# Dilated-attention loads and the inverse's stores issued from GpSimd, query halves exchanged, head norm over two iterations

## The chip, the cores and the metric

The kernel runs on one core of a Trainium2 chip. The metric is the device time of one execution in microseconds (us). Engines are named as in the profile: PE (TensorE matmul), DVE (VectorE), ACT (ScalarE), POOL (GpSimd), SP (SyncE, which here only issues DMAs). ACTq, SPq and POOLq are DMA issues that stand in those engines' instruction streams. Each engine executes its instructions in the order of the program.

## The reference, cut to what matters

Two transformer blocks on one sequence of 1024 tokens, width 1024. The second block's mixer has two halves, both 512 wide, which the kernel runs side by side.

```python
# half 1: dilated attention, 8 heads of 64; three branches (window, dilation) share one softmax
DILATED_BRANCHES = ((128, 1), (512, 4), (2048, 16))
outs = [_dilated_branch(qh, kh, vh, w, d) for (w, d) in DILATED_BRANCHES]
m_all = maximum of the three m
num = sum(exp(m - m_all)[..., None] * acc for (m, l, acc) in outs)
den = sum(exp(m - m_all) * l for (m, l, acc) in outs)
# half 2: RWKV7, 8 heads of 64, a recurrence over the 1024 tokens
sa    = einsum('bhij,bhj->bhi', state, kk_t)
state = state * w_t - sa[..., None] * b_t + v_t[..., None] * k_t
y     = einsum('bhij,bhj->bhi', state, r_t)
# then a norm of y within each head, gain, bias, bonus and gate
yn = (y - mean) * lax.rsqrt(var + GN_EPS)
out = (yn * gn_w + gn_b + bonus) * g
mixed = concatenate([rms_norm(attn), out]) @ w_out      # then the feed-forward layer
```

## The kernel before, in words

The change lies in `mixers`, from about 1320 to 1725 us of the span. Ahead of it are block one and the projections of block two; behind it `finish` (the output projection, the feed-forward layer), whose first matmuls (tile x) need every dilated head and every norm of the mixer's first half of tokens, and whose further ones need the rest.

The dilated half is done as eight heads' passes, t = 0 to 7 (two attention heads of 64 channels each, and one half of the queries; passes 4 to 7 see 1024 keys instead of 512). `dil_load(t)` brings keys (dk) and values (dqv); `dil_load_q(x)` brings 256 queries (dq), for x = 0 to 15, two to a pass, into one of two buffers. A pass has 4 blocks of 128 queries and in each two heads (m): score matmuls into sc (L1288, L1289; 192 in the whole stage), a masked maximum on DVE (L1292), the exponential on ACT (L1298), transposes (tp, L254), products with the values (pv, L431). The result is stored to da_d (L1309). These loads and stores stand in ACT's stream.

The RWKV half is done as eight units, n = 0 to 7. For each: `rwkv_local` (call it L0 to L7; PE L1326 and L1337) makes matrices AT, stores them to at_d and loads them back as Al in another layout (SPq L1344, L1346). `rwkv_inverse` inverts triangles on POOL: a copy, then 31 steps of one multiplication (Ut, L1363) and one subtraction (U, L1365), and four stores to ut_d (SPq L1368). `rwkv_solve` (V0 to V7) loads ut_d as TB (SPq L1408, a single buffer), copies OFF on POOL (L1402), and runs six groups of matmuls (L1417, L1445, L1446, L1454) for two quads of chunks. `rwkv_state` (S) is a chain of eight small steps, a matmul (L1480) and an addition on DVE (L1482) each. `rwkv_norm` transposes, centres, squares, takes the reciprocal root on POOL (rstdh, L172), scales (L1519), transposes back (tile e), gates and stores to rw_d. Local, inverse, solve, state and norm of five units (n, n-1, n-2, n-3, n-4) run in one iteration of the loop; AT, RHS and RQ have three buffers, so a unit's local needs the buffers of the solve three units back.

All this stands in a block whose instruction order is worked out when the program is built, from the code and a model of the engines; so a changed line moves instructions on every engine. The order is fixed then; nothing is reordered at run time.

Of the kernel before, what the change touches and what calls it, by code (L numbers as in the profile page):

```python
# [86 lines left out]
class Build:  # L87
# [1158 lines left out]
    def dil_load(self, t):  # L1246

        i, n = t % 4, (t // 4 + 1) * 512
        v = self.dpool.tile([128, NT, 128], F32, name="dqv")
        K = [self.dpool.tile([128, S], F32R, name="dk", bufs=2) for _ in range(2)]  # L1250
        for m in range(2):
            self.nc.scalar.dma_start(K[m][:, :n].bitcast(F32), self.dqk_d[i][:, 2 + m, :n])
        self.nc.scalar.dma_start(v[:, :n // 128], self.dv_d[i][:n].rearrange("(t p) c -> p t c", p=128))
        self.dil_kv[t] = K, v

    def dil_load_q(self, x):

        i, g = x // 2 % 4, x // 8 * 2 + x % 2
        qs = self.dil_q[x] = self.dpool.tile([128, 2, 2, 256], F32R, name="dq", bufs=2)
        for s in range(2):  # L1260
            src = self.dqk_d[i][s * 64:s * 64 + 64, 0:2, g * 256:g * 256 + 256]
            for h in range(2):
                self.nc.scalar.dma_start(qs[h * 64:h * 64 + 64, :, s].bitcast(F32), src)

    def dilated(self, t):
# [222 lines left out]
    def rwkv_norm(self, n, p, hf):  # L1488

        nc = self.nc  # L1490
        t0 = hf * 512
# [7 lines left out]
        ps = None
        yield 1.0  # L1500

        def keep(i, n, x):
            nonlocal ps
            ps = x
        self.transposes([YT[:, j * 128:j * 128 + 128] for j in range(4)], keep, tag=tag)
# [13 lines left out]
        nc.vector.tensor_mul(y3(y), y3(y), rs[:, :, None].to_broadcast([128, 8, 64]))  # L1519
        self.transposes([y[:, j * 128:j * 128 + 128] for j in range(4)], keep, tag=tag)  # L1520
        nc.vector.tensor_mul(wg, ps, wg)
        nc.vector.tensor_add(wg, wg, bg)
# [529 lines left out]
```

## Time and profile before

| | |
|---|---|
| time, median of 3 runs | 2496.82 us (2484.91 to 2497.03) |
| the profiled execution's own time | 2490.68 us |
| its span in the profile | 2488.8 us, mean granted TensorE clock 0.977 |
| busy in the span | PE 95%, DVE 60%, ACT 41%, POOL 12% |
| PE idle before an instruction, 1384 to 1435 us | 9.04 and 6.35 us at two places |

The times of the rows further down are microseconds from the start of the span of this one execution. A busy PE there is not PE at its peak, since matmuls are pipelined and their ends modelled; the distance between the starts of two groups is the better measure of a group's price.

### The profile page before, as it was taken

The numbers are of one execution on the slowest core, as the hardware profiler recorded it, in microseconds if no ns is written. First come the engines' busy times: TensorE is split into PE (matmuls) and PEld (weight loads), VectorE is DVE, ScalarE is ACT, GpSimd is POOL, SyncE is SP. The second block draws the span as 40 slices with busy tenths as digits, with TensorE's granted clock in tenths as the row PEclk, the third lists the DMA queues.
The fourth block names the chain that finished last, engine by engine and source line by source line (L and its number), as shares of the span: only waits on it lengthen the run. The fifth ranks groups of instructions, "written<-read, shape, count | busy, mean of one in ns | idle before, by whom it ended". The sixth has DMA issues, their size and how long they took to land.

```text
span 2488.8 us, 38514 instructions
## 1 busy us (share of the span) xinstructions
PE 2354.3 (95%) x14272; PEld 2080.8 (84%) x14272; DVE 1493.3 (60%) x3189; ACT 1016.8 (41%) x2212; POOL 286.5 (12%) x678
## 2 busy tenths in 40 slices
PE   7999999999999999899999699989999999899997
PEld 6989998898887799788899688988987878678776
DVE  5534375555445545376663366757676666678888
ACT  4323343434442235233342344445665444443333
POOL 1100000000001000111203645331000000000001
PEclk9999999999999999999999899999999999999999
DMA  3144222312214432245467676534455444443222
GB/s 126 45 141 137 78 59 71 91 41 90 78 52 169 152 123 81 64 118 161 131 185 201 167 171 182 148 94 149 153 161 178 147 128 140 153 135 127 68 78 100
DMA packets 370188, 303.38 MB, mean 122 GB/s; under 512 B 124304, under 2 KB 303632, under 8 KB 370000
## 3 DMA queue, kind: packets, MB, share of 16 engines
q1 hardware_dynamic: 343888, 272.60, 36.6%
q10 hardware_dynamic: 25472, 26.22, 3.6%
q8 instruction: 113, 1.85, 0.3%
q0 software_dynamic: 640, 2.10, 0.2%
q14 instruction: 75, 0.61, 0.1%
HBM read 208.82 MB, written 91.23 MB: 121 GB/s over the span
## 4 chain that ended last, share of the span: by engine, by line
PE 71%; DMA 10%; DVE 9%; ACT 4%; issue 3%; POOL 2%; SPq 1%; ACTq 0%; DVEq 0%; POOLq 0%
PE pj L199 33%; PE x L199 7%; PE z L199 5%; PE pv L431 4%; PE y L199 4%; PE tp L254 3%; DMA wr<-w_ffn_up 3%; DVE w L181 2%; PE ua L199 2%; PE Z L1417 1%; PE sc L778 1%; DMA Al<-at_d 1%; ACT w L163 1%; PE ub L199 1%; DMA wr<-w_out 1%
## 5 line engine op out<-in xcount | busy, mean ns | idle before, releaser
L199 PE MATMUL pj<-w,hT_hi 128*128 128x256 f32 (+2 forms) x2496 | 526.6, 305 | 11.3 <-DVE c L165 6.2
L199 PEld LDWEIGHTS pj<-w,hT_hi 128*128 128x128 f32 x2496 | 409.8, 193 | 18.5 <-DVE c L165 7.5
L199 PE MATMUL pj<-hT_hi,w 128*128 128x512 f32 (+1 forms) x1216 | 394.3, 399 | 9.8 <-DVE tg L922 6.4
L199 PE MATMUL pj<-w,hT_lo 128*128 128x256 f32 (+2 forms) x1248 | 373.6, 300 | 0.0
L181 DVE TENSOR_TENSOR w<-wr,w 128x1024 fp32r<-128x1024 f32 (+4 forms) x339 | 273.1, 832 | 114.1 <-ACT w L163 113.2
L163 ACT ACTIVATE w<-wr 128x1024 fp32r<-128x1024 f32 (+4 forms) x335 | 236.1, 740 | 233.3 <-PE z L199 69.0
L199 PEld LDWEIGHTS pj<-hT_hi,w 128*128 128x128 f32 (+1 forms) x1216 | 227.0, 188 | 60.9 <-ACT w L163 4.8
L199 PEld LDWEIGHTS pj<-w,hT_lo 128*128 128x128 f32 x1248 | 240.2, 192 | 1.0 <-issue 0.5
L199 PE MATMUL pj<-hT_lo,w 128*128 128x512 f32 (+1 forms) x608 | 240.0, 395 | 0.0
L172 POOL TENSOR_TENSOR rstd<-rs_t,mhalf 128x1 f32<-128x1 f32 x88 | 62.3, 712 | 1482.2 <-DVE rs_t L171 1429.0
L199 PE MATMUL z<-w 128*128 128x512 f32 x720 | 168.5, 394 | 5.6 <-DVE c L1927 4.8
L199 PEld LDWEIGHTS z<-w 128*128 128x128 f32 x720 | 136.5, 190 | 36.1 <-issue 4.3
L199 PE MATMUL y<-w 128*128 128x512 f32 x624 | 148.4, 397 | 15.4 <-ACT w L163 9.0
L199 PEld LDWEIGHTS y<-w 128*128 128x128 f32 x624 | 118.8, 192 | 43.7 <-ACT w L163 10.2
L199 PE MATMUL ua<-T,w 128*128 128x512 f32 x576 | 139.3, 393 | 5.3 <-DVE o L1859 2.3
L199 PEld LDWEIGHTS ua<-T,w 128*128 128x128 f32 x576 | 107.3, 189 | 32.3 <-issue 6.3
L199 PEld LDWEIGHTS pj<-hT_lo,w 128*128 128x128 f32 (+1 forms) x608 | 114.8, 189 | 22.7 <-issue 0.2
L408 DVE TENSOR_REDUCE mx<-sc 128x1 f32<-128x128 f32 (+7 forms) x96 | 70.9, 754 | 101.5 <-PE sc L416 100.9
L254 PE MATMUL tp<-ident,p 128*128 128x128 f32 x576 | 98.4, 279 | 6.8 <-ACT pt L163 5.7
L199 PE MATMUL x<-w,mix_hi 128*128 128x256 f32 x512 | 92.6, 284 | 0.0
L199 PE MATMUL x<-B,w 128*128 128x512 f32 x384 | 88.3, 390 | 0.0
L412 ACT ACTIVATE p<-sc,mx 128x128 f32<-128x128 f32 (+7 forms) x96 | 70.7, 739 | 36.5 <-DVE mx L409 34.6
(448 smaller groups left out, 4423.5 us busy)
## 6 DMA issues: line engine op xcount, KB each, us to landing
wr<-w_ffn_up SPq DMA_DIRECT2D x48, 512.0 KB, 4.5
wr<-u_d SPq DMA_DIRECT2D x32, 512.0 KB, 3.3
wr<-w_ffn_down SPq DMA_DIRECT2D x32, 512.0 KB, 3.6
wr<-w_in SPq DMA_DIRECT2D x28, 512.0 KB, 4.0
wr<-w_in_first SPq DMA_DIRECT2D x64, 192.0 KB, 2.7
u_d<-o SPq DMA_DIRECT2D x48, 256.0 KB, 3.0
tg<-tg_d SPq DMA_DIRECT2D x32, 256.0 KB, 2.8
x_d<-x SPq DMA_DIRECT2D x16, 512.0 KB, 3.9
```

Source lines behind the costliest of these rows:

```text
L163: self.nc.scalar.activation(out, in_, AF.Copy)
L172: nc.gpsimd.tensor_tensor(out, t, self.mhalf[:, :ss.shape[-1]], op=OP.pow)
L181: self.nc.vector.tensor_sub(lo, x, hi.bitcast(F32))
L199: self.nc.tensor.matmul(ps, a, b, start=start, stop=stop, **({"skip_group_check": True} if onto else {}))
L254: self.nc.tensor.transpose(tp[:, j * 128:j * 128 + 128], s, ident)
L408: nc.vector.tensor_reduce(mx, sc[:, :n], axis=AX, op=OP.max)
L412: nc.scalar.activation(p[:, :n], sc[:, :n], AF.Exp, bias=mx, scale=scale, accum_out=s)
L431: self.nc.tensor.matmul(o[:, :w], pts[j], V[:, j], start=j == 0, stop=j == nb - 1)
L778: nc.tensor.matmul(o, qn, KN[:, c0:c0 + w], start=True, stop=False)
L1417: mm(ps[:, j * 128:j * 128 + 128], lhs(c), rhs(c, j), start=True, stop=True)
```

## The change

Five edits. The loads of dk, dqv and dq and the stores of da_d are issued by POOL instead of ACT, and the stores of ut_d by POOL instead of SP. Keys come as tiles of 512 with four buffers, so that one DMA brings both heads' keys and the next pass's keys may be loaded early. A dq load is three DMAs instead of four: the 128 rows as they are, and the two halves exchanged; the second score matmul takes the exchanged copy. The load of the next 256 queries stands behind the first block's first scores, and da_d's store of a pass stands in the next pass. The norm is cut in two: `rwkv_norm` up to the reciprocal root in one iteration, `rwkv_out` (load of wb, scale, transposes, gate, store) in the next; the loop has one iteration more. Beside `rwkv_out` the diff's new helpers `centre` and `gate` hold DVE work that stood in `rwkv_norm`.

```diff
 def dil_load(self, t):
-    v = self.dpool.tile([128, NT, 128], F32, name="dqv")
-    K = [self.dpool.tile([128, S], F32R, name="dk", bufs=2) for _ in range(2)]
-    for m in range(2):
-        self.nc.scalar.dma_start(K[m][:, :n].bitcast(F32), self.dqk_d[i][:, 2 + m, :n])
-    self.nc.scalar.dma_start(v[:, :n // 128], self.dv_d[i][:n].rearrange("(t p) c -> p t c", p=128))
+    for c in range(n):
+        K.append(self.dpool.tile([128, 2, 512], F32R, name="dk", bufs=4))
+        self.nc.gpsimd.dma_start(K[c].bitcast(F32), self.dqk_d[i][:, 2:4, c * 512:c * 512 + 512])
+    v = self.dpool.tile([128, NT, 128], F32, name="dqv")
+    self.nc.gpsimd.dma_start(v[:, :n * 4], self.dv_d[i][:n * 512].rearrange("(t p) c -> p t c", p=128))
 def dil_load_q(self, x):
-    for s in range(2):
-        src = self.dqk_d[i][s * 64:s * 64 + 64, 0:2, g * 256:g * 256 + 256]
-        for h in range(2):
-            self.nc.scalar.dma_start(qs[h * 64:h * 64 + 64, :, s].bitcast(F32), src)
+    src = self.dqk_d[i][:, 0:2, g * 256:g * 256 + 256]
+    self.nc.gpsimd.dma_start(qs[:, 0].bitcast(F32), src)
+    for h in (0, 64):
+        self.nc.gpsimd.dma_start(qs[h:h + 64, 1].bitcast(F32), src[64 - h:128 - h])
 def dilated(self, t):
-                if x < 15:
-                    self.dil_load_q(x + 1)
-            if qb % 4 == 1 and t < 7:
-                self.dil_load(t + 1)
+            if qb % 4 == 1:
+                if t < 7:
+                    self.dil_load(t + 1)
+                if t > 0:
+                    self.dil_store.pop()()
-                    nc.tensor.matmul(sc[:, :w], q2[:, m, 0, q0:q0 + 128], K[m][:, c0:c0 + w], start=True, stop=False)
-                    nc.tensor.matmul(sc[:, :w], q2[:, m, 1, q0:q0 + 128], K[m][:, c0:c0 + w], start=False, stop=True)
+                    k = K[c0 // 512][:, m, c0 % 512:c0 % 512 + w]
+                    nc.tensor.matmul(sc[:, :w], q2[:, 0, m, q0:q0 + 128], k, start=True, stop=False)
+                    nc.tensor.matmul(sc[:, :w], q2[:, 1, m, q0:q0 + 128], k, start=False, stop=True)
-                            nc.scalar.dma_start(dst.rearrange("(t p) c -> p t c", p=128), o)
+                            put = lambda: nc.gpsimd.dma_start(dst.rearrange("(t p) c -> p t c", p=128), o)
+                            put() if t == 7 else self.dil_store.append(put)
                 yield back, 0.25 + n * 0.0036
+                if qb % 2 == 0 and m == 0 and x < 15:
+                    self.dil_load_q(x + 1)
 def rwkv_inverse(self, n, p, hf):
         for g in range(4):
-            nc.sync.dma_start(ut_d.rearrange("c b (i g) t -> g (c b) i t", g=4)[g], U[g * 32:g * 32 + 32])
+            nc.gpsimd.dma_start(ut_d.rearrange("c b (i g) t -> g (c b) i t", g=4)[g], U[g * 32:g * 32 + 32])
 def rwkv_norm(self, n, p, hf):
-        self.load(wb, self.ch_d["wb"][p][:, :, t0:t0 + 512])
-        ET = lambda: self.lpool.tile([128, 512], F32, name="e", bufs=2)
+        ET = lambda: self.lpool.tile([128, 512], F32, name="e", bufs=3)
...
-        rs = self.norm_rows(var, 64, GN_EPS, "h")
+        self.YN[n] = y, self.norm_rows(var, 64, GN_EPS, "h")
+        yield 0.5
+    def rwkv_out(self, n, p, hf):
+        y, rs = self.YN.pop(n)
+        self.load(wb, self.ch_d["wb"][p][:, :, t0:t0 + 512])
+        nc.vector.tensor_mul(y3, y3, rs[:, :, None].to_broadcast([128, 8, 64]))
...
+        nc.sync.dma_start(self.rw_d[p][:, t0:t0 + 512], wg)
 def mixers(self, dense, proj):
-            for n in range(len(units) + 4):
+            for n in range(len(units) + 5):
-                for back, f, cost in ((4, self.rwkv_norm, 4.5), (3, self.rwkv_state, 3.2), (2, self.rwkv_solve, 20.0),
+                for back, f, cost in ((5, self.rwkv_out, 3.6), (4, self.rwkv_norm, 1.5), (3, self.rwkv_state, 3.2), (2, self.rwkv_solve, 20.0),
                                       (1, self.rwkv_inverse, 9.4), (0, self.rwkv_local, 12.0)):
```

In the changed program the lines stand up to six lines lower: L1291/L1292 are the score matmuls, L1252, L1254, L1262 and L1264 the loads, L1312 the da_d store, L1369/L1371 the inverse's steps, L1374 the ut_d stores, L1423 to L1460 the solve, L1486/L1490 the state.

POOL's stream of before, in unit 1's inverse around its eighth step (U, Ut and Al are the inverse's tiles; what is awaited stands in brackets, Pool being the step before):

```order
L1365 TENSOR_TENSOR U<-U,Ut 128x2x25 [waits Pool_49]
L1363 TENSOR_TENSOR Ut<-U,Al 128x2x24 [waits Pool_49]
L1365 TENSOR_TENSOR U<-U,Ut 128x2x24 [waits Pool_49]
L1363 TENSOR_TENSOR Ut<-U,Al 128x3x23 [waits Pool_49]
L1365 TENSOR_TENSOR U<-U,Ut 128x3x23 [waits Pool_49]
L1363 TENSOR_TENSOR Ut<-U,Al 128x3x22 [waits Pool_49]
L1365 TENSOR_TENSOR U<-U,Ut 128x3x22 [waits Pool_49]
```

POOL's stream of the changed program at the same step:

```order
L1369 TENSOR_TENSOR Ut<-U,Al 128x2x24 [waits Pool_49]
L1252 DMA dk<-dqk_d_11166 128x2x512 [waits DMASW4_49,DVE_49]
L1254 DMA dqv<-dv_d_11170 128x4x128 [waits DMAHW4_49,DMASW5_49,DMAHW5_49,DVE_49,PE_49]
L1262 DMA dq<-dqk_d_11166 128x2x256 [waits DMAHW2_49,DMAHW5_49,DMAHW0_49,DMAHW7_49,DMASW6_49,DVE_49]
L1264 DMA dq<-dqk_d_11166 64x2x256 [waits DMASW7_49]
L1264 DMA dq<-dqk_d_11166 64x2x256
L1262 DMA dq<-dqk_d_11166 128x2x256
L1264 DMA dq<-dqk_d_11166 64x2x256 x2
L1252 DMA dk<-dqk_d_11167 128x2x512 [waits DMAHW6_49,DMASW4_49]
L1254 DMA dqv<-dv_d_11171 128x4x128 [waits DMAHW6_49,DMAHW1_49,DMAHW7_49,DMASW5_49,Activation_49]
L1371 TENSOR_TENSOR U<-U,Ut 128x2x24 [waits Pool_49]
L1252 DMA dk<-dqk_d_11168 128x2x512 [waits DMASW6_49]
```

The loads of the first pass and of the first 512 queries now stand between the two halves of one step of unit 1's inverse, and the rest of that inverse stands behind them. Up to its end 36 more such issues follow between its steps, and those of dq, dqv and da_d mostly wait for PE or ACT to be done with an earlier part of a head.

The end of unit 1's inverse on POOL, before (unit 2's inverse follows directly; the stores stand on SP):

```order
L1363 TENSOR_TENSOR Ut<-U,Al 128x8 [waits Pool_49]
L1365 TENSOR_TENSOR U<-U,Ut 128x8 [waits Pool_49]
L1363 TENSOR_TENSOR Ut<-U,Al 128x31 [waits DMAHW6_49,Pool_49]
L1365 TENSOR_TENSOR U<-U,Ut 128x31 [waits Pool_49]
L1363 TENSOR_TENSOR Ut<-U,Al 128x30 [waits Pool_49]
```

The same place in the changed program:

```order
L1369 TENSOR_TENSOR Ut<-U,Al 128x8 [waits Pool_49]
L1371 TENSOR_TENSOR U<-U,Ut 128x8 [waits Pool_49]
L1262 DMA dq<-dqk_d_11167 128x2x256 [waits DMASW3_49,DMASW2_49,PE_49]
L1264 DMA dq<-dqk_d_11167 64x2x256
L1264 DMA dq<-dqk_d_11167 64x2x256 [waits DMASW4_49]
L1374 DMA ut_d_13397<-U 256x1x32 [waits DMASW5_49,Pool_49]
L1374 DMA ut_d_13397<-U 256x1x32 [waits DMASW6_49]
L1374 DMA ut_d_13397<-U 256x1x32 [waits DMASW7_49]
L1374 DMA ut_d_13397<-U 256x1x32 [waits DMASW0_49]
L1369 TENSOR_TENSOR Ut<-U,Al 128x31 [waits DMAHW5_49]
```

The stores of unit 1's inverse (ut_d) now stand behind the dq load of x = 10, whose wait on PE is for the buffer of x = 8, that is for the 80th of the 192 score matmuls.

PE's stream where the last solve, V7, begins, before (S_1, S_2 belong to the states of units 5 and 6; RHS and TB to the solve):

```order
L1288 MATMUL sc<-dk,dq 128x512
L1289 MATMUL sc<-dk,dq 128x512
L1417 MATMUL Z<-RHS_13386,TB_13390 128x128 x4
L254 MATMUL tp<-ident,p 128x128 x2
L431 MATMUL pv<-dqv,pt 128x64 x4
L1480 MATMUL Y<-S_2_16402,M_14658 128x128
L1484 MATMUL Y<-R_14657,S_1_17515 128x64
L254 MATMUL Z<-ident,YT 128x128
L1417 MATMUL Z<-RHS_13386,TB_13390 128x128 x4
L431 MATMUL pv<-dqv,pt 128x64 x2
L254 MATMUL tp<-ident,p 128x128 x4
L1288 MATMUL sc<-dk,dq 128x512
```

And in the changed program:

```order
L1486 MATMUL Y<-S_2_17760,M_14658 128x128
L1490 MATMUL Y<-R_14656,S_2_17760 128x64
L1486 MATMUL Y<-S_2_17795,M_14658 128x128
L1423 MATMUL Z<-RHS_13386,TB_13390 128x128 x8
L1490 MATMUL Y<-R_14656,S_2_17795 128x64
L1423 MATMUL Z<-z_17710,OFF_13387 128x128 x4
L1423 MATMUL Z<-z_17717,OFF_13387 128x128 x4
L1490 MATMUL Y<-R_14656,S_2_17832 128x64
L1423 MATMUL Z<-RHS_13386,TB_13390 128x128 x8
L254 MATMUL Z<-ident,e 128x128 x4
L1423 MATMUL Z<-RQ_13389,gn_13398 128x128 x4
L1423 MATMUL Z<-RQ_13389,gn_13399 128x128 x4
```

Before, scores, transposes and products of the last passes stand between the matmuls of V7 and of two states. Now no instruction of a dilated pass is left there. The same shift over the whole stage: score matmuls of the 192 that PE has been given before each solve begins, and the PE work from one mark to the next (counted from the order, each kind of matmul at its start-to-start time in the trace of before):

| | V0 | V1 | V2 | V3 | V4 | V5 | V6 | V7 |
|---|---|---|---|---|---|---|---|---|
| scores given ahead, before | 0 | 28 | 50 | 76 | 102 | 124 | 140 | 156 |
| scores given ahead, changed | 0 | 92 | 118 | 144 | 172 | 192 | 192 | 192 |
| PE work from here to the next mark, before, us | 28.9 | 32.9 | 35.8 | 38.7 | 36.5 | 25.4 | 25.9 | 57.0 |
| PE work from here to the next mark, changed, us | 66.9 | 39.8 | 39.9 | 39.4 | 34.8 | 23.8 | 17.3 | 19.8 |

The last column ends where finish's first matmuls (x) begin. L3 stands between V0 and V1 in both programs, L7 between V4 and V5.

## Rows read from the trace of the kernel before

**Rows 1.** The page, busy time and share of each engine.

```profile
PE 2354.3 (95%) x14272; PEld 2080.8 (84%) x14272; DVE 1493.3 (60%) x3189; ACT 1016.8 (41%) x2212; POOL 286.5 (12%) x678
```

**Rows 2.** Windows: length, busy (instructions) PE PEld DVE ACT POOL, clock, DMA, GB/s.

```profile
1384.00:1435.00 51.00, 33.37 (x253) 31.42 (x253) 20.71 (x87) 17.69 (x59) 28.39 (x99) 0.83 0.67 165
1435.00:1660.00 225.00, 204.29 (x1688) 199.15 (x1688) 140.79 (x493) 104.95 (x284) 104.15 (x331) 0.95 0.59 157
1660.00:1721.00 61.00, 58.04 (x473) 53.76 (x473) 47.53 (x160) 34.21 (x84) 7.45 (x7) 1.00 0.29 92
```

**Rows 3.** Timeline of PE, first solve: start, length, instruction, idle before.

```profile
1384.35 1.13 PE L1417 MATMUL Z<-RHS,TB 128*128 128x128 f32 x8
...
1396.46 0.77 PE L1288 MATMUL sc<-dk,dq 128*128 128x256 f32 x2 [9.04 <-DMA dq<-dqk_d]
1403.57 0.77 PE L1289 MATMUL sc<-dk,dq 128*128 128x256 f32 x2 [6.35 <-DMA dqv<-dv_d]
```

**Rows 4.** Timeline of ACT in the same stretch.

```profile
1390.87 8.03 ACTq L1263 DMA_DIRECT2D dq<-dqk_d  x8
...
1399.59 0.38 ACT L1338 ACTIVATE RHS<-Z 128x256 f32<-128x256 f32 x1 [16.49 <-DMA dq<-dqk_d]
```

**Rows 5.** Timeline of PE, marks from V1 to the last norm.

```profile
1435.34 0.89 PE L1417 MATMUL Z<-RHS,TB 128*128 128x128 f32 x6
...
1488.02 1.22 PE L1417 MATMUL Z<-RQ,gn 128*128 128x128 f32 x4 [3.53 <-ACT HN L1433]
...
1595.41 0.61 PE L1337 MATMUL Z<-v,BT 128*128 128x64 f32 x4
...
1642.05 2.08 PE L1417 MATMUL Z<-RHS,TB 128*128 128x128 f32 x8 [9.31 <-DVE RHS L1426]
...
1660.61 1.05 PE L1417 MATMUL Z<-RHS,TB 128*128 128x128 f32 x8
...
1692.21 0.56 PE L1484 MATMUL Y<-R,S 128*128 128x64 f32 x4
...
1712.15 0.33 PE L1484 MATMUL Y<-R,S 128*128 128x64 f32 x2
...
1718.88 0.66 PE L254 MATMUL Y<-ident,e 128*128 128x128 f32 x4
```

**Rows 6.** Timeline of POOL, ends of inverses 1 (start), 6 and 7.

```profile
1371.69 0.24 POOL L1363 TENSOR_TENSOR Ut<-U,Al 128x31 f32<-128x31 f32 x1
...
1595.71 0.22 POOL L1365 TENSOR_TENSOR U<-U,Ut 128x8 f32<-128x8 f32 x1
...
1615.92 0.24 POOL L1363 TENSOR_TENSOR Ut<-U,Al 128x31 f32<-128x31 f32 x1 [12.54 <-DMA Al<-at_d]
...
1638.69 0.22 POOL L1365 TENSOR_TENSOR U<-U,Ut 128x8 f32<-128x8 f32 x1
```

**Rows 7.** Timeline of SP behind the last inverse.

```profile
1638.94 2.53 SPq L1368 DMA_DIRECT2D ut_d<-U  x4
1644.15 1.81 SPq L1408 DMA_DIRECT2D TB<-ut_d  x4
```

**Rows 8.** Waits, 1320 to 1721 us: total, times, longest.

```profile
DVE e L1519 <- POOL rstdh L172: 23.2, 5, 11.5
```

**Rows 9.** Tile tg_d: DMA issues on POOL, ns min/median/max.

```profile
L847 POOL DMA_DIRECT2D tg_d<-ev x8: 542/582/1017, 731.9 to 794.1; - x8
```

**Rows 10.** Tile Al: the inverse's first kind of step, ns min/median/max.

```profile
L1363 POOL TENSOR_TENSOR Ut<-U,Al x248: 208/280/731, 1349.4 to 1638.4; 128x60 f32<-128x60 f32 x12, 128x54 f32<-128x54 f32 x8, 128x66 f32<-128x66 f32 x8, 128x28 f32<-128x28 f32 x8
```

**Rows 11.** DMA issues, 1300 to 1721 us: size, median us to landing.

```profile
dq<-dqk_d ACTq DMA_DIRECT2D x64, 128.0 KB, 4.2
...
TB<-ut_d SPq DMA_DIRECT2D x32, 32.0 KB, 2.2
```

**Rows 12.** Lines, 1384 to 1721 us: busy, mean ns, idle before.

```profile
L1298 ACT ACTIVATE p<-p,nb 128x128 f32<-128x128 f32 (+7 forms) x64 | 49.4, 773 | 27.0 <-DVE nb L1296 22.9 <-DVE S L1482 2.7 <-DVE rs L1302 1.2
...
L172 POOL TENSOR_TENSOR rstdh<-rs_th,mhalf 128x8 f32<-128x8 f32 x8 | 13.2, 1644 | 61.6 <-DVE rs_th L171 61.6
```

More of the change, by code (lines that the diff above doesn't have):

```diff
@@ L1246, in dil_load @@
     def dil_load(self, t):
-        i, n = t % 4, (t // 4 + 1) * 512
+        i, n = t % 4, t // 4 + 1
+        K = []
+        for c in range(n):
+            K.append(self.dpool.tile([128, 2, 512], F32R, name="dk", bufs=4))
+            self.nc.gpsimd.dma_start(K[c].bitcast(F32), self.dqk_d[i][:, 2:4, c * 512:c * 512 + 512])
         v = self.dpool.tile([128, NT, 128], F32, name="dqv")
-        K = [self.dpool.tile([128, S], F32R, name="dk", bufs=2) for _ in range(2)]
-        for m in range(2):
-            self.nc.scalar.dma_start(K[m][:, :n].bitcast(F32), self.dqk_d[i][:, 2 + m, :n])
-        self.nc.scalar.dma_start(v[:, :n // 128], self.dv_d[i][:n].rearrange("(t p) c -> p t c", p=128))
+        self.nc.gpsimd.dma_start(v[:, :n * 4], self.dv_d[i][:n * 512].rearrange("(t p) c -> p t c", p=128))
         self.dil_kv[t] = K, v
@@ L1490, in rwkv_norm @@
         nc = self.nc
-        t0 = hf * 512
         YT = self.YT.pop(n)
-        tag = "Y" if n > 6 else "Z"
-        wb = self.lpool.tile([128, 2, 512], F32, name="wb", bufs=1)
-        self.load(wb, self.ch_d["wb"][p][:, :, t0:t0 + 512])
-        wg, bg = wb[:, 0], wb[:, 1]
-        ET = lambda: self.lpool.tile([128, 512], F32, name="e", bufs=2)
[L1499 to L1505, printed above, removed]
+        ET = lambda: self.lpool.tile([128, 512], F32, name="e", bufs=3)
+        yield 0.5
         y = ET()
@@ L1508, in rwkv_norm, with centre @@
         mean = self.small.tile([128, 8], F32, name="mean")
-        nc.vector.tensor_reduce(mean, y3(ps), axis=AX, op=OP.add)
-        nc.vector.tensor_scalar(mean, mean, -1.0 / 64, None, op0=OP.mult)
-        nc.vector.tensor_add(y3(y), y3(ps), mean[:, :, None].to_broadcast([128, 8, 64]))
+        def centre(i, n, ps):
+            nc.vector.tensor_reduce(mean, y3(ps), axis=AX, op=OP.add)
+            nc.vector.tensor_scalar(mean, mean, -1.0 / 64, None, op0=OP.mult)
+            nc.vector.tensor_add(y3(y), y3(ps), mean[:, :, None].to_broadcast([128, 8, 64]))
+        self.transposes([YT[:, j * 128:j * 128 + 128] for j in range(4)], centre, tag="Y" if n > 6 else "Z")
         yield 0.5
@@ L1516, in rwkv_norm, with gate @@
         nc.vector.tensor_reduce(var, y3(sq), axis=AX, op=OP.add)
-        rs = self.norm_rows(var, 64, GN_EPS, "h")
-        yield 2.0
[L1519 to L1522, printed above, removed]
+        self.YN[n] = y, self.norm_rows(var, 64, GN_EPS, "h")
+        yield 0.5
+    def rwkv_out(self, n, p, hf):
+        nc = self.nc
+        t0 = hf * 512
+        y, rs = self.YN.pop(n)
+        wb = self.lpool.tile([128, 2, 512], F32, name="wb", bufs=1)
+        self.load(wb, self.ch_d["wb"][p][:, :, t0:t0 + 512])
+        wg, bg = wb[:, 0], wb[:, 1]
+        y3 = y.rearrange("p (a c) -> p a c", c=64)
+        yield 0.5
+        nc.vector.tensor_mul(y3, y3, rs[:, :, None].to_broadcast([128, 8, 64]))
+        yield 2.0
+        def gate(i, n, ps):
+            nc.vector.tensor_mul(wg, ps, wg)
+            nc.vector.tensor_add(wg, wg, bg)
+        self.transposes([y[:, j * 128:j * 128 + 128] for j in range(4)], gate, tag="Y" if n > 6 else "Z")
+        yield 1.0
         nc.sync.dma_start(self.rw_d[p][:, t0:t0 + 512], wg)
-        yield 0.5
+        yield 0.1
     def mixers(self, dense, proj):
@@ L1561, in mixers @@
             zero += self.gn
-            self.S0, self.Al, self.YT = {}, {}, {}
+            self.S0, self.Al, self.YT, self.YN = {}, {}, {}, {}
             def clear():
@@ L1575, in mixers @@
             self.gate = self.rwkv_load1(0, *units[0]).ins
-            self.dil_kv, self.dil_q = {}, {}
-            for n in range(len(units) + 4):
+            self.dil_kv, self.dil_q, self.dil_store = {}, {}, []
+            for n in range(len(units) + 5):
                 st_ = []
```

## The prediction

> **What bounds the kernel now.** I read the page's busy shares first: PE is busy for 95% of the span [rows 1], so time can come only from places where PE waits or runs at the lower clock. Then the windows of the mixers' stage [rows 2]: 1384 to 1435 us is the loose stretch (PE busy 33.37 of 51 us, granted clock 0.83), 1435 to 1660 is nearly full (204.29 of 225), 1660 to 1721 is full (58.04 of 61). Then PE's timeline for the holes. In the first solve PE stands 9.04 us for the first dq and 6.35 us at the second score matmul [rows 3]; in the latter case dqv is named, but ACT's stream shows what is behind it: eight dq issues take 8.03 us in ACT's own stream, and ACT's evacuation of RHS comes 16.49 us late behind them [rows 4]. Later holes are 3.53 us, where the solve waits for ACT's HN, and 9.31 us, where it waits for DVE's RHS [rows 5]; DVE was late there because it stood in the norm's scaling (tile e) for POOL's reciprocal root, in all 23.2 us in five waits, the longest 11.5 [rows 8]. The end of the stage is a chain for the last unit: the end of L7 at 1596.0, inverse 7 from 1615.92 to 1638.9, V7 from 1660.61, state 7 from 1692.21 to 1712.4, the last norm's transposes at 1718.88 [rows 5, 6]. Between the end of inverse 7 and V7 PE had other work to do; that work was the dilated passes.
>
> **What the change removes.** The 15.4 us of PE's two early waits [rows 3] go in large part: POOL issues dk and dq, and ACT is free to evacuate V0's groups. V0 can run alone and be done at about 1400 instead of 1423. The split norm takes the 9.31 us hole away (the root is read an iteration later), and ACT, with no DMA waits in its stream, the 3.53. That is 28 us at most, and it is a gain only if nothing else sets the end. dq's three DMAs instead of four move the same bytes; the matmuls' number and widths stay. The later da_d store is covered by the next pass. I cost these at nothing; without cover an issue is 0.58 us [rows 9].
>
> **What it adds, and where.** The order rows show the price. The issues of the heads up to x = 10 stand inside unit 1's inverse, and the ut_d store of that inverse stands behind the dq load that waits for the 80th score matmul. So V1 can't start until PE has done four passes and half of the fifth. PE gets 92 of the 192 score matmuls before V1 instead of 28, and the tail gets none.
>
> Step 1, the start of V1. The first dq issue was at 1390.87, since it waits for stores of the projections [rows 4], and it lands 4.2 us later [rows 11]; with the first scores x = 0 begins at about 1397. An x has four score-and-softmax units. ACT's exponential takes 0.77 us of each [rows 12], with its other part of the work about 1.0 us, so an x costs at least 4.4 us when nothing waits. But a dq load may start only when the buffer of two x before is free: three issues (1.7 us at 0.58 [rows 9]; up to 3.1 at the longest, 1.02) and 4.2 of landing, 5.9 to 7.3. With two buffers the pace lies between 4.4 (loads hidden) and 7.3 (nothing hidden but the first unit, 1.1 + 6.2); since POOL also holds dqv, da_d and inverse steps between the loads, I take 6.5. Eight of them bring x = 8 to 1397 + 52 = 1449; x = 8 has keys beyond 512, two score pieces to a unit, and takes 9: 1458. Then three dq and four ut_d issues (4.1 us), the stores' landing and TB's issue and landing: from the end of an inverse to TB landed is 1644.15 + 1.81 + 2.2 - 1638.9 = 9.3 us today [rows 6, 7, 11], of which 2.53 is the issue. 1458 + 1.7 + 2.3 + 7 = 1469, and some waits more: 1472 for V1, against 1435.34 before [rows 5]. Bounds: PE's work alone, 66.9 us from 1384.35, gives 1451 and with V0's solitary waits about 1460; the pace 7.3 gives 1480.
>
> Step 2, from V1 to the end of L7. By the table in the section on the change this is 153.9 us of PE work now, 143.9 before, which took 1596.0 - 1435.3 = 160.7 us: 16.8 us of waits and of lower clock. If the waits for ACT and the like vanish half of these stay, if not all: 153.9 + 8 to 17. I take 12: 166, so L7 ends at 1638, 42 us later than before. What could have been made up is done beforehand by the passes already.
>
> Step 3, the tail. From L7's end to inverse 7 19.9 us (the at_d stores and Al's load [rows 5, 6]; the same DMAs from SP now, and the same two loads of w_out among them), the inverse 23.0 [rows 6], to TB 9.3 (4 issues of 0.58 on POOL instead of 2.53 on SP, so no different). In these 52 us PE has V5 and V6, 41 us, which fit. V7 then runs alone: today 28.4 us among other work, 11.6 if only its 104 matmuls counted; nearer to the lower, since the six groups of two quads overlap: 15. State 7 took 20.2 us among others' work [rows 5]; its eight steps, each a matmul and an addition on DVE, I estimate at 10 alone. The norm as today, 1718.88 - 1712.4 = 6.5 [rows 5]. Sum 19.9 + 23 + 9.3 + 15 + 10 + 6.5 = 84, so 1722. And PE has little to do there: in the stretch where it was busy 65% the granted clock was 0.83 [rows 2], that is, part of the time at 1.2 instead of 2.4 GHz; V7 and state 7 have the same thinness (20 us of work in 32). At that clock 20 us become 24, and some of the same falls on the heads' solitary stretch: 7 in all. The last norm's transposes come at 1729 instead of 1718.9, **+10 us**. Behind them nothing changes.
>
> The profiled execution took 2490.68 us with a span of 2488.8, and lies 6.1 under the median of the runs. So 2501 for such an execution and **2507** as a median.
>
> **Rivals.**
> (a) Faster. The heads' loads are hidden (pace 4.4 to 5), V1 starts at 1460, the rest of the waits is gone (153.9 + 8 = 162, L7 ends at 1622), and the tail is as short as its parts allow (V7 12, state 8, no clock loss: 79). The last norm at 1701, 18 us sooner: 2479. For it speaks that 28 us of waits go; against it that all of the passes' work is spent where units 1 to 4 could have run, and that 52 us of the tail are DMAs and POOL, which the change doesn't shorten. It decides from a pace of 5 us downward. Chance 0.20.
> (b) No change: the same with V1 at 1466 and a tail of 82: 1466 + 163 + 82 = 1711 and a few us of lower clock, 1715 to 1720: 2493 to 2498. This is also where it ends if ACT's issues were no cost to begin with and the passes only changed places. Chance 0.25.
> (c) POOL becomes the bound of the first passes. No POOL issue here has more than 128 contiguous pieces (tg_d, 0.58 us [rows 9]); counted from the code a dq load has 512, a dqv 512 to 1024, a da_d store 512, a dk tile 256, the four ut_d stores 1024. If the issue costs as much per piece, a dq load is 2.3 us, the 36 and more issues ahead of ut_d of unit 1 cost some 56 us beside 22 of inverse, the pace is 8.5, x = 8 ends at 1474 and V1 starts at 1488: 16 later than forecast, and with later units' longer issues +18: 2525. Against it: the issue's time between 542 and 1017 ns does not look like counting pieces. Chance 0.12.
> (d) POOL's issues are stretched by DVE's work. An inverse step, 280 ns at the median, took up to 731 [rows 10], so something now and then holds POOL for 2.6 times as long. If issues were held so, 0.58 becomes 1.5, a dq load 4.5 + 4.2, pace 8.7: again about 2525. Chance 0.08. The Trainium skill (SBUF — State Buffer, section "SBUF: two separate sides") speaks against the change here: DMAs issued by GpSimd have their descriptors written by it, and it cannot write them while VectorE holds the port both share; 620 ns alone became some 3100 there. By that an estimate would be 9.3 us for one dq load's issues, a pace above 13, and some 45 us more than my sum; the eight tg_d issues, at most 1017 ns, don't show it, but they stood in another stage.
> The forecast itself, +3 to +20: 0.35.
>
> **Numbers.** A change of 0.5%, 12.5 us, is about what can be told from none. Faster: (a), 0.20. Within: (b) and the lower part of the forecast's range, 0.40. Slower: its upper part, (c) and (d), 0.40. The range 2482 to 2540 leaves out the better half of (a) and the worse ends of (c) and (d).
>
> **What would show it.** Right: no wait of 9 and 6 us in the first solve and V0 done near 1400; heads' scores without any solve until V1 at 1465 to 1480, with PE waiting for dq between them; ut_d of unit 1 issued after x = 8's scores; no hole over 5 us at a solve for DVE's RHS; PE with holes and a lower clock from V6 to the last norm, at 1722 to 1738. Wrong: V1 before 1460, or a tail from L7's end to the last norm under 78 us, would make it faster; dq or ut_d issues on POOL over 1.5 us each would make it slower than the range's middle, and a pace over 8 us would show where.

## The result

The changed kernel takes 2513.73 us (median of 6 runs, 2509.36 to 2517.05), the kernel before 2496.93 (6 runs beside them, 2484.91 to 2500.22). The ratio is 1.0073, 95% interval 1.0058 to 1.0089: slower by 0.7%. The profiled execution took 2509.36 us with a span of 2507.5, 18.7 more than that of before. The forecast was 2507 and a range of 2482 to 2540. The late V1 and the bare end that it forecast are there; the end is longer than forecast, some of the waits that make up its steps are others than it said, and one edit was mispriced altogether.

### The profile page after: what moved, and what is told of

The parts are those of the page before. It is cut to its first block, busy times and chain, and to the rows that moved or that the text cites. A ratio compares the mean times of both kernels' runs of the same rounds, so it can differ in the third digit from the quotient of the medians.

```text
span 2507.5 us, 38574 instructions
## 1 busy us (share of the span) xinstructions
PE 2366.7 (94%) x14272; PEld 2084.0 (83%) x14272; DVE 1498.5 (60%) x3189; ACT 1020.3 (41%) x2212; POOL 358.2 (14%) x786
## 4 chain that ended last, share of the span: by engine, by line
PE 70%; DVE 10%; DMA 9%; ACT 4%; issue 3%; POOL 2%; SPq 1%; DVEq 0%; ACTq 0%; POOLq 0%
PE pj L199 33%; PE x L199 7%; PE z L199 5%; PE y L199 5%; PE pv L431 4%; DMA wr<-w_ffn_up 3%; PE tp L254 3%; PE Z L1423 2%; DVE w L181 2%; PE sc L778 1%; ACT w L163 1%; DMA TB<-ut_d 1%; PE sc L810 1%; PE ua L199 1%; PE Z L1332 1%
## 5 line engine op out<-in xcount | busy, mean ns | idle before, releaser
L199 PE MATMUL pj<-hT_hi,w 128*128 128x512 f32 (+1 forms) x1216 | 394.2, 399 | 10.9 <-DVE tg L922 6.9
L181 DVE TENSOR_TENSOR w<-wr,w 128x1024 fp32r<-128x1024 f32 (+4 forms) x339 | 273.2, 832 | 113.1 <-ACT w L163 112.4
L199 PE MATMUL y<-w 128*128 128x512 f32 x624 | 149.0, 398 | 14.4 <-ACT w L163 9.4
```

What stands on the lines that cost most here:

```text
L181: self.nc.vector.tensor_sub(lo, x, hi.bitcast(F32))
L199: self.nc.tensor.matmul(ps, a, b, start=start, stop=stop, **({"skip_group_check": True} if onto else {}))
```

## The profile after

The page first. Against [rows 1] PE has 12 us more in its busy time for the same number of matmuls, and POOL has 72 us and 108 instructions more: these are the new DMA issues.

```profile
PE 2366.7 (94%) x14272; PEld 2084.0 (83%) x14272; DVE 1498.5 (60%) x3189; ACT 1020.3 (41%) x2212; POOL 358.2 (14%) x786
```

PE's timeline answers to [rows 3] and [rows 5]: the first solve, V1's first group, the end of L7, V7's first group, steps of the last state, the last norm's transposes.

```profile
1380.65 3.07 PE L1423 MATMUL Z<-RHS,TB 128*128 128x128 f32 x16 [1.91 <-DMA TB<-ut_d]
...
1391.51 0.66 PE L1291 MATMUL sc<-dk,dq 128*128 128x256 f32 x2 [3.49 <-DMA dq<-dqk_d]
...
1470.97 2.02 PE L1423 MATMUL Z<-RHS,TB 128*128 128x128 f32 x16 [1.63 <-DMA TB<-ut_d]
...
1637.45 1.00 PE L1343 MATMUL Z<-v,BT 128*128 128x64 f32 x8
...
1697.38 3.62 PE L1423 MATMUL Z<-RHS,TB 128*128 128x128 f32 x16
...
1717.86 0.49 PE L1486 MATMUL Y<-S,M 128*128 128x128 f32 x2 [0.41 <-DVE YT L1491]
1720.74 0.69 PE L1490 MATMUL Y<-R,S 128*128 128x64 f32 x2 [2.39 <-DVE S L1488]
1721.22 0.74 PE L1486 MATMUL Y<-S,M 128*128 128x128 f32 x2
...
1743.36 1.12 PE L254 MATMUL Y<-ident,e 128*128 128x128 f32 x4 [5.81 <-DVE e L1528]
```

The early holes of 9.04 and 6.35 us are one of 3.49. V1 starts at 1471.0 instead of 1435.3, 35.7 later. From there to the end of L7 it takes 167.5 us instead of 160.7, and from there to the last norm's transposes 104.9 instead of 122.9; so these come at 1743.4 instead of 1718.9, 24.5 later. Of that 5.8 us are made up in `finish`.

POOL's timeline between V0 and V1 shows why V1 is late: dq loads of x = 2, 3 and 10 with POOL's wait for scores ahead of them, and ut_d's stores of unit 1's inverse behind the last.

```profile
1400.51 0.75 POOL L1262 DMA_DIRECT2D dq<-dqk_d  x1 [6.12 <-PE sc L1292]
...
1410.71 0.75 POOL L1262 DMA_DIRECT2D dq<-dqk_d  x1 [3.22 <-PE sc L1292]
...
1457.40 0.75 POOL L1262 DMA_DIRECT2D dq<-dqk_d  x1 [2.50 <-PE sc L1292]
...
1459.34 1.76 POOL L1374 DMA_DIRECT2D ut_d<-U  x3
```

Unit 1's inverse, which began at 1371.7 as before [rows 6], ended at 1454.9: 83 us instead of 24. Between its steps stand 46 issues, which take 31.9 us themselves, and the waits ahead of them; dq's waits for scores among these are 18.2 us in seven (an eighth, of 2.50 us, stands behind the last step). So of the 59 us of delay more than half is the issues' own time on POOL, and less than a third the waits for PE.

Windows (columns as in [rows 2]) from V0's end to V1, to the end of L7, to V7, and to the last norm:

```profile
1401.00:1471.00 70.00, 61.70 (x454) 53.66 (x453) 43.14 (x205) 43.46 (x136) 45.04 (x101) 1.00 0.75 200
1471.00:1639.00 168.00, 157.98 (x1315) 153.38 (x1316) 105.42 (x356) 78.42 (x191) 111.92 (x315) 0.98 0.47 123
1639.00:1697.00 58.00, 49.97 (x384) 46.66 (x384) 33.94 (x90) 17.32 (x44) 43.27 (x118) 0.90 0.36 105
1697.00:1744.00 47.00, 28.68 (x164) 24.72 (x164) 24.17 (x66) 13.15 (x37) 6.31 (x6) 0.68 0.32 107
```

PE is well filled up to L7. The largest loss is in the last row: 47 us with 28.68 busy and a granted clock of 0.68, where before the same end was full at 1.00 [rows 2].

The tiles' issues on POOL (ns min/median/max), which answer to [rows 9]: dq, dqv and ut_d, from three answers.

```profile
L1264 POOL DMA_DIRECT2D dq<-dqk_d x32: 601/605/643, 1383.0 to 1584.6; - x32
L1262 POOL DMA_DIRECT2D dq<-dqk_d x16: 707/739/793, 1382.3 to 1583.0; - x16
...
L1254 POOL DMA_DIRECT2D dqv<-dv_d x8: 772/857/954, 1381.3 to 1553.4; - x8
...
L1374 POOL DMA_DIRECT2D ut_d<-U x32: 561/603/649, 1369.4 to 1690.6; - x32
```

No such issue takes over 954 ns, whether it has 128 contiguous pieces or 1024.

## The experiments

Every kernel's order of instructions is worked out anew from its code, so a difference between two kernels is that of the edit and of the order that comes with it. "Over" and "under" are against the median of the kernel before, run beside them: 2490.86 us for e1 to e4, 2488.93 for e5, e8, e9 and e10, 2491.74 for the others. The marks V1 and last norm are read from one execution of each kernel.

| kernel | loads issued by | ut_d by | norm, tiles | median us | ratio, 95% | V1 starts | last norm |
|---|---|---|---|---|---|---|---|
| before | ACT | SP | old | 2496.93 | | 1435.3 | 1718.9 |
| changed | POOL | POOL | new | 2513.73 | 1.0073, 1.0058 to 1.0089 | 1471.0 | 1743.4 |
| e1 | ACT | POOL | new | 2479.99 | 0.9955, 0.9939 to 0.9971 | 1432.7 | 1708.4 |
| e2 | POOL | SP | new | 2495.56 | 1.0015, 1.0005 to 1.0026 | 1466.1 | 1723.4 |
| e3 | ACT | SP | new norm, old tiles | 2487.54 | 0.9984, 0.9971 to 0.9996 | 1432.0 | 1718.6 |
| e4 | SP | POOL | new | 2462.70 | 0.9882, 0.9864 to 0.9901 | 1427.4 | 1694.8 |
| e5 | ACT | POOL | old | 2477.56 | 0.9953, 0.9932 to 0.9975 | 1429.6 | 1706.3 |
| e7 | ACT | SP | new | 2503.85 | 1.0044, 1.0029 to 1.0060 | 1435.5 | 1729.9 |
| e8 | POOL, dq and dk 3 buffers | POOL | new | 2506.86 | 1.0074, 1.0055 to 1.0092 | 1480.5 | 1741.1 |
| e9 | SP | SP | new | 2481.41 | 0.9966, 0.9953 to 0.9978 | 1422.3 | 1710.0 |
| e10 | SP | SP | old | 2494.53 | 1.0019, 1.0006 to 1.0032 | 1421.8 | 1727.7 |
| e11 | SP | POOL | new tiles, old norm | 2473.32 | 0.9926, 0.9908 to 0.9943 | 1426.2 | 1701.1 |
| e14 | dq SP, others POOL | POOL | new | 2467.75 | 0.9894, 0.9876 to 0.9912 | 1429.7 | 1692.4 |
| e15 | dq ACT, others POOL | POOL | new | 2456.68 | 0.9856, 0.9836 to 0.9876 | 1425.8 | 1685.9 |

**Theory and rivals.** The theory was that unit 1's inverse and its store stand behind the heads' loads in POOL's stream, so PE spends the passes early and the end is bare. Rival 1: the ut_d stores on POOL delay each unit. Rival 2: the norm's extra iteration lengthens the end.

**e1, loads back to ACT.** In the changed kernel:

```diff
-    self.nc.gpsimd.dma_start(K[c]...)        # and dqv, dq (two lines), da_d
+    self.nc.scalar.dma_start(K[c]...)
```

> The changed kernel with dk, dqv, dq and da_d issued by ACT again; ut_d stores on POOL, new tiles and the split norm stay. In its order PE has 30 score matmuls before V1 (28 before, 92 changed) and 32 left behind V7's start. Theory (unit 1's inverse and its ut_d store stand behind dq waits in POOL's stream, so the passes are spent early and the tail is bare): V1 back at 1430 to 1440 us, time 0 to 10 us under before. Rival 1 (ut_d on POOL is what delays each unit): 10 to 17 us over before, as changed. Rival 2 (the norm's extra iteration lengthens the end): 10 to 17 us over before.

10.9 us under, V1 at 1432.7. The gain is a little over what was expected. Both rivals fall, since ut_d on POOL and the cut norm are both in it. The loads' place costs the changed kernel 1.0073 against 0.9955, some 29 us.

**e2, only ut_d back to SP.**

```diff
-            nc.gpsimd.dma_start(ut_d.rearrange(...)[g], U[g * 32:g * 32 + 32])
+            nc.sync.dma_start(ut_d.rearrange(...)[g], U[g * 32:g * 32 + 32])
```

> The changed kernel with only the ut_d stores back on SP. Loads stay on POOL. Its order gives 68 score matmuls before V1 and none behind V7's start. Theory: unit 1's inverse still has the loads of seven x between its steps, so V1 starts near 1450 and only a third to a half of the loss goes: 5 to 13 us over before. Rival 1 (ut_d on POOL is the cost): no slower than before. Rival 2 (norm): 10 to 17 over before.

4.7 us over (interval of the ratio 1.0005 to 1.0026), just under the 5 to 13 that the theory gave, and more than rival 1 allowed. V1 came at 1466.1, not near 1450: the inverse ended at 1446.4, but SP waited 13.0 us for the landing of ut_d's stores, as the row of PE's timeline shows at its other end. From 1454 to 1462 the last of these stores' small packets ran among 1.15 MB of packets of the loads that POOL had issued; what held them isn't shown.

```profile
1466.10 3.75 PE L1423 MATMUL Z<-RHS,TB 128*128 128x128 f32 x16 [6.30 <-DMA TB<-ut_d]
```

So the start of V1 isn't all of the loss. It is 4.9 us sooner than in the changed kernel, but the end of L7 (1618.5) and the last norm are 20 us sooner: inverse 2 no longer stands behind the dq load of x = 10 and begins at 1446.5 instead of 1462.2, and the later inverses with it.

**e3, the cut norm alone,** in the kernel before (`rwkv_norm` and `rwkv_out` as in the change, the loop one longer).

> The kernel before with the norm cut in two alone. Theory: the 9.31 us hole at a solve behind POOL's reciprocal root goes, and most of it reaches the end: 3 to 10 us under before, no wait of DVE for the root over 3 us. Rival 1: the same. Rival 2 (the norm's extra iteration costs at the end): 5 to 17 us over before, with the last norm's transposes later after the last state than the 6.5 us of before.

3.3 us under, the lower end of the theory's span, but not for its reason: the waits of DVE for the root are all still there.

```profile
DVE e L1522 <- POOL rstdh L172: 24.3, 5, 11.4
```

Compare [rows 8]: 23.2 in five, longest 11.5. POOL's stream has the root behind inverse steps either way, and PE still had holes of 9.5 and 6.7 us. Cutting the function in two doesn't by itself move the root on POOL.

**e4, loads to SP** (as e1, with `sync`).

> The changed kernel with dk, dqv, dq and da_d issued by SP; ut_d stores on POOL, split norm kept. Its order gives 30 score matmuls before V1 and 36 behind V7's start. Theory: ACT and POOL both stay free of load waits, the two early holes shrink, the tail keeps its cover: 8 to 20 us under before. If SP's own in-order waits hold the RWKV loads behind dq, as POOL's did, it is 0 to 10 over before. Rival 1 (ut_d on POOL): 10 to 17 over before. Rival 2 (norm): 10 to 17 over before.

28 us under: with ACT and POOL both free of the loads' waits, V0 is done at 1401, V1 starts at 1427 and V7 has score matmuls beside it. The expected span ended at 20 under.

**e5, ut_d to POOL alone,** in the kernel before (the line of e2 the other way).

> The kernel before with only the ut_d stores moved to POOL. Its order gives 28 score matmuls before V1 and 32 behind V7's start. If this edit by itself helps (SP no longer stands for an inverse before its next loads): 3 to 9 us under before. If it is neutral and the 11 us of the run with loads on ACT came from the new tiles, the third dq DMA less and the norm: 0 to 2 us from before. If POOL's four issues per inverse cost: 2 to 6 over.

11.4 us under, from one line, more than any case expected. The waits in SP's own stream tell where it comes from. The kernel before, 1384 to 1721 us:

```profile
SPq L1368 <- POOL U L1365: 44.9, 5, 15.1
```

SP stood 44.9 us in five waits for POOL to finish an inverse before it could issue ut_d's store, with the next units' loads queued behind it. With the store in POOL's stream this wait has no place: it follows the inverse's last step anyhow. A part of it comes back at the next load of ut_d, where SP waits 34.7 us in nine for the stores to land (20.6 in seven before). But at_d's stores and Al's loads come sooner: from the end of a unit's local to the issue of Al's load it is 20.6 us in all for units 2 to 7, 33.0 in the kernel before, and POOL's waits for Al, 81.5 us in seven before, are 68.0 in seven.

**e8, three buffers for dq and for dk,** in the changed kernel.

```diff
-        K.append(self.dpool.tile([128, 2, 512], F32R, name="dk", bufs=4))
+        K.append(self.dpool.tile([128, 2, 512], F32R, name="dk", bufs=3))
-        qs = self.dil_q[x] = self.dpool.tile([128, 2, 2, 256], F32R, name="dq", bufs=2)
+        qs = self.dil_q[x] = self.dpool.tile([128, 2, 2, 256], F32R, name="dq", bufs=3)
```

> The changed kernel with three buffers for dq and three for dk instead of two and four; all queues as changed. Theory (what costs is how much of the passes stands ahead of unit 1's ut_d in POOL's stream, not how long one load takes): its order has 96 score matmuls before V1, so it is as slow as the changed kernel or slower, 12 to 25 us over before, though PE waits less for dq. Rival (the pace of the dq loads is the cost): 0 to 10 us over before.

18 us over. A third buffer for the late tile doesn't help (dk lost one of four at the same time): 96 scores instead of 92 stand ahead of V1, which comes at 1480.5, and POOL's waits for scores at dq are 23.2 us (20.7 in the changed kernel). So the amount of passes in front of ut_d counts, not how long a load takes.

**e9, loads and ut_d on SP** (e4 and e2 together).

> As the run with the loads on SP, and the ut_d stores on SP too, so POOL issues nothing. If ut_d on POOL is a part of that run's 28 us: 14 to 24 us under before. If not: 25 to 31 under.

7.5 us under, so ut_d's place is worth some 20 of e4's 28. Here SP does what POOL did in the changed kernel, and one place shows a whole chain. PE's longest hole, 19.55 us at a score matmul, names DVE; DVE stood 21.70 us for POOL's root; POOL has the root behind the first step of inverse 6, which waited 18.68 us for Al; and in SP's timeline the at_d store and Al's load of that unit stand behind ut_d's store of unit 5, for which SP waited 12.9 us. (L6 had ended at 1526. The rest is the load itself: from its issue at 1538.87 to the step that it releases it is 15.9 us.) First PE, then DVE, POOL and SP of the same kernel:

```profile
1557.72 0.58 PE L1291 MATMUL sc<-dk,dq 128*128 128x256 f32 x1 [19.55 <-DVE mx L1295]
```

```profile
1556.67 0.73 DVE L1528 TENSOR_TENSOR e<-e,rstdh 128x512 f32<-128x512 f32 x1 [21.70 <-POOL rstdh L172]
```

```profile
1554.80 0.24 POOL L1369 TENSOR_TENSOR Ut<-U,Al 128x31 f32<-128x31 f32 x1 [18.68 <-DMA Al<-at_d]
1554.99 1.64 POOL L172 TENSOR_TENSOR rstdh<-rs_th,mhalf 128x8 f32<-128x8 f32 x1
```

```profile
1531.63 2.54 SPq L1374 DMA_DIRECT2D ut_d<-U  x4
...
1534.96 2.09 SPq L1350 DMA_DIRECT2D at_d<-AT  x4
...
1538.87 0.55 SPq L1352 DMA_DIRECT2D Al<-at_d  x1
```

**e10, the loads on SP alone,** in the kernel before.

> The kernel before with nothing but dk, dqv, dq and da_d issued by SP instead of ACT; old tiles, four dq DMAs, whole norm. If the gain of the run with the loads on SP is ACT's freedom from issues: 12 to 24 us under before, with no wait of ACT's RHS for dq of 16 us. If it needs the early keys (four dk buffers) and the norm: 0 to 10 under.

5.6 us over, outside both cases. V1 came early (1421.8), and the gain was lost again: three of PE's holes, 4.2, 6.5 and 5.4 us, stand at the first scores of passes 1, 2 and 3, the first two of them for dk; another of 7.2 stands at a state. The old tiles have no buffer in which the next pass's keys could come early, and DVE's waits for the root are 19.9 us as in the kernel before.

**e14, dq on SP, the other loads on POOL.**

```diff
-        self.nc.gpsimd.dma_start(qs[:, 0].bitcast(F32), src)      # and the two halves
+        self.nc.sync.dma_start(qs[:, 0].bitcast(F32), src)
```

> The changed kernel with the dq loads alone taken off POOL (to SP); dk, dqv, da_d and ut_d stay on POOL. Its order has 38 score matmuls before V1 and 20 left behind V7's start. Theory narrowed (the dq loads' waits for PE inside unit 1's inverse are the cost, not that heads' loads are on POOL at all): 10 to 25 us under before, V1 at 1425 to 1445. If any head's load on POOL costs (dqv and da_d wait for PE and ACT too): 0 to 15 over before.

24 us under, V1 at 1429.7: as the narrowed theory had it. Of the heads' transfers on POOL it is dq that does the harm; dk, dqv and da_d can stay. Unit 1's inverse takes 44 us there, 83 with dq. Not all of these 39 us are waits for PE, as that theory said: 18.2 are, and dq's 30 issues among the steps take some 19.5 (ten loads of 0.74 + 2 x 0.605).

**e15, dq on ACT, the other loads on POOL.**

> As the run before it, with the dq loads on ACT. Theory narrowed: V1 at 1425 to 1445 again, but ACT stands for its dq issues in the first solve, so 5 to 15 us under before and less than with dq on SP. If any head's load on POOL costs: 0 to 15 over.

35 us under, the fastest kernel of the study, and a miss: less than e14 was expected. The early hole is as large as ever (14.55 us for the first dq), but behind it PE is full.

```profile
1384.00:1425.00 41.00, 32.99 (x257) 31.92 (x257) 21.01 (x89) 18.75 (x61) 21.03 (x65) 0.84 0.85 213
1425.00:1570.00 145.00, 144.81 (x1249) 141.89 (x1248) 106.04 (x384) 79.05 (x218) 107.77 (x311) 1.00 0.70 182
1570.00:1686.00 116.00, 111.42 (x905) 107.27 (x904) 83.69 (x268) 60.26 (x147) 49.96 (x122) 0.96 0.37 112
```

144.81 us of 145 are busy at the full clock, and DVE waits 0.6 us in all for the root (2.3 in e14, 11.1 in e4, 23.2 before [rows 8]). POOL waits for Al only 17.7 us, against 50.1 in e4: with the dk, dqv and da_d issues between its steps an inverse takes 28 to 36 us (unit 1's 43), where the solves V1 to V5 start 33 to 38 us apart, and Al is mostly there when it begins. So the issues on POOL fill time in which it stood. Why ACT beats SP for dq by some 11 us was not taken apart further.

**e11, e4 with the norm whole.**

> The kernel with the loads on SP and ut_d on POOL, with the norm of before in one piece. If the cut norm's gain is that of the run with the norm alone (3 us): 22 to 28 us under before. If the cut matters more where nothing else waits: 10 to 21 under.

18.4 us under, so the cut norm is worth some 10 us there (0.9926 against 0.9882), against 3 by itself. DVE's waits for the root are not what it saves: 11.1 us in e4, 10.1 here. By what else it gains was not tested.

**e7, all queues as before,** new tiles and cut norm only.

> The changed kernel with all queues as before (loads and da_d on ACT, ut_d on SP): only new tiles, three dq DMAs, later load and store, cut norm. Beside the run with ut_d on POOL too (11 us under before) it prices that store: if the store's move alone gives its 11 us (as in the kernel before), this is 2 us over to 5 under before; if the tiles and the norm give the 11: 8 to 14 under.

12.1 us over, which none of the cases had. Beside e1 (10.9 under) the ut_d store's move is worth 23 us in this company. The trace shows where the new tiles cost with the old queues: in three places a solve stands for ACT (holes of PE of 5.79, 5.14 and 5.47 us), and each time an issue of dk, of da_d or of dq stands in ACT's stream just ahead of what the solve waits for. The first of them, on ACT and then on PE:

```profile
1450.75 0.37 ACTq L1252 DMA_DIRECT2D dk<-dqk_d  x1
1451.17 0.38 ACT L1438 ACTIVATE gn<-Z 64x256 f32<-64x256 f32 x1 [5.43 <-DMA Al<-at_d]
```

```profile
1452.53 0.80 PE L1423 MATMUL Z<-RQ,gn 128*128 128x128 f32 x2 [5.79 <-ACT HN L1439]
```

It is the fault of the changed kernel on a third engine. That these 16.4 us are all of the loss was not tested.

## Why the prediction was right, and where it was not

**V0 and the early holes: right.** V0's last group began at 1400.4; forecast near 1400. The two holes became one of 3.49 us.

**Step 1, V1: right in the sum.** 1471.0 against 1472. x = 8 began at 1450.3 (forecast 1449). The pace, from the dq issue of x = 2 at 1400.51 to that of x = 10 at 1457.40, is 7.1 us and not 6.5, near the upper bound of 7.3; the first scores, at 1391.5, were 5.5 us earlier than assumed, and it is luck that the two errors cancel. The reason given for the pace is not what the trace shows: it was to be set by the dq loads, with PE waiting for them. From 1401 to 1471 PE waits 1.1 us in all for dq and is busy 61.70 of 70 us at the full clock; POOL waits for the scores, not PE for the loads. That the passes stand ahead of V1 is shown: take dq out of POOL's stream (e1, e14, e15) and V1 is back at 1426 to 1433; give dq another buffer and leave it there (e8), and V1 is later still.

**Step 2, to the end of L7: right in number.** 1638.5 - 1471.0 = 167.5, forecast 166. But the 12 us of waits in it were to be what is left of waits for ACT and the like; in the trace solves wait there 11.1 us in four for ut_d, that is for POOL's late inverses, and for ACT 0.2 us. The row for the whole stage, 1380 to 1745:

```profile
PE Z L1423 <- DMA TB<-ut_d: 13.9, 6, 5.3
```

**Step 3, the tail: the right cause, undersized.** 1743.4 - 1638.5 = 104.9 us; forecast 84, with 7 for the clock 91. By parts, measured against forecast: to inverse 7's first step at 1660.8 22.3 (19.9), the inverse 28 (23.0: a root, a da_d issue and two OFF copies stand between its steps), to V7 9 (9.3), V7 to its last transposes 18.5 (15), the state to 1736.8 20.9 (10), the norm 6.6 (6.5).

The first part is near its forecast by luck. The forecast had inverse 7 wait for at_d's stores and Al's load. Al's load was issued at 1639.66, and POOL was still in inverse 6; inverse 7 begins right behind that one's stores and waits for nothing.

```profile
1656.94 0.22 POOL L1371 TENSOR_TENSOR U<-U,Ut 128x8 f32<-128x8 f32 x1
1657.56 1.23 POOL L1374 DMA_DIRECT2D ut_d<-U  x2 [0.41 <-POOL U L1371]
1659.64 1.14 POOL L1374 DMA_DIRECT2D ut_d<-U  x2 [0.85 <-issue]
1660.76 0.28 POOL L1369 TENSOR_TENSOR Ut<-U,Al 128x31 f32<-128x31 f32 x1
```

So unit 1's late inverse reaches the end through POOL's stream too: POOL's only wait for Al is unit 0's, 15.4 us, and each later inverse follows the one before it.

The term that failed most is state 7: "its eight steps, each a matmul and an addition on DVE, I estimate at 10 alone". It isn't alone on DVE. Two of its additions with nothing of others between them are 1.6 us apart (1733.11 to 1734.71, at the lower clock); its seven additions, from 1715.85 to 1734.71, take 18.9 us. Between them DVE does some 6.5 us of work of `finish` (splits of weights, L181; scaling of the heads' output, L1670) and some 5.7 of the norms of units 5 and 6, and stands 2.40 us at L1532 (the view names no cause; by its time it is the load of wb issued at 1727.21). PE is near half clock meanwhile: the windows 1716 to 1737 and 1737 to 1744 were granted 0.58 and 0.50.

```profile
1720.40 0.28 DVE L1488 TENSOR_TENSOR S<-Y,PT 128x128 f32<-128x128 f32 x1
1720.60 0.42 DVE L181 TENSOR_TENSOR w<-wr,w 128x256 fp32r<-128x256 f32 x1
...
1722.32 0.22 DVE L1491 TENSOR_TENSOR YT<-Y,PY 128x64 f32<-128x64 f32 x1
1722.45 0.48 DVE L1670 TENSOR_SCALAR da<-da,rstd 128x512 f32<-128x512 f32 x1
...
1722.90 0.28 DVE L1488 TENSOR_TENSOR S<-Y,PT 128x128 f32<-128x128 f32 x1
```

The work so done early is part of what `finish` needs, and would explain some of the 5.8 us made up later; that was not tested. "Behind them nothing changes" was wrong by them. They hide a part of the error: the last norm is 14.4 us later than the forecast 1729, the profiled execution only 8.4 longer than the forecast 2501.

**What the change removes: one term missing, one reason wrong.** The move of ut_d to POOL was costed at nothing but a delay. e5 shows it to be a gain of 11 us by itself and of 20 to 23 in company (e9 to e4, e7 to e1): SP's 44.9 us of waiting at that store were in the trace of before, in the waits of SP's own stream, a view that the prediction did not use. In the changed kernel the same edit costs some 12 to 14 (e2 to the change), because POOL's stream there isn't free. And the 9.31 us hole was to go "since the root is read an iteration later". It did go (DVE waits 2.9 us in all for the root), but e3 has the cut and keeps the waits. The root waits where it stands behind an inverse's step that itself waits for Al: POOL's waits for Al are 84.6 us in e3 and 15.4 in the changed kernel, where the inverses are so slow that Al is there from unit 1 on. These waits alone don't decide: e7, with 85.8 us of them and the cut norm, has only 7.2 us of waits for the root. What else decides, the place that the order gives the root in POOL's stream among others, was not tested.

**The rivals.** (a) and (b) needed V1 at 1460 and 1466 and a tail of 79 and 82; V1 came at 1471.0 and the tail took 104.9. (c) and (d), POOL issues priced by pieces or stretched: the longest of 108 is 954 ns, a dq load 0.74 + 2 x 0.605 = 1.95 us rather than 2.3 by pieces or 4.5 by stretch. dq's transfers landed after 6.4 us at the median where the sum took 4.2 [rows 11], but not because POOL issued them: the same three land after 6.4 from SP (e4) and 6.1 from ACT (e1). The Trainium skill (SBUF — State Buffer, section "SBUF: two separate sides") warns that a DMA issued by GpSimd waits for its descriptors while VectorE holds the port that both share, 620 ns alone becoming some 3100. The trace shows it neither on these issues nor on their landings, with DVE busy 43 us of the 70 in which 42 of the 108 stand; how much of DVE's work holds that port isn't on record.

## What to carry to other kernels

A DMA issue that waits is a wait of everything behind it in its engine's stream: before moving one, read the waits of the stream it leaves (what it holds there is the gain) and of the stream it joins (what stands behind its wait is the loss). A store in its producer's own stream waits for nothing new, as long as nothing that waits stands between the producer and it (e5 gained 11 us; e2 to the change lost 12 to 14). A load that waits for a consumer's buffer must not stand inside another chain's work, and count its issue time too: in unit 1's inverse the issues cost more than the waits. Work used up early to fill a hole is missed at the end of a latency chain, where PE here also ran at a granted clock of 0.68.

## What was not expected of the hardware

DMA issues on GpSimd took 0.56 to 0.95 us by kind, and hardly by the number of contiguous pieces: dqv's issues with 512 and with 1024 pieces (counted from the code) all lie between 772 and 954 ns, and ut_d's with 256 pieces at 603. Transfers of dq issued there landed after 6.4 us at the median, at a DMA share of 0.75 of the stretch; from SP the same landed after 6.4 (e4) and 7.5 (e14), from ACT after 6.1 (e1) and 5.1 (e15). So the issuing engine doesn't make the difference to the 4.2 of before; whether the new cut of the load or the moment of it does stays open.
